# Side jobs of a feed-forward block cut into small pieces, part of them moved to the second block

## The chip, the cores and the metric

The kernel runs on one core of a Trainium2 chip. The metric is the device time of one execution in microseconds (us), smaller is better; the median of 3 runs before the change is 2384.21 us (2381.77 to 2387.19).

The engines of the core are called as in the profile: PE (TensorE, matrix products; PEld is its loading of the stationary operand), DVE (VectorE), ACT (ScalarE), POOL (GpSimd), SP (SyncE, which here only issues DMAs). Each engine works through its own queue in order. Line numbers such as L526 are those of the kernel before.

## The reference

A trunk of four layers over one sequence of 512 positions and 1024 channels, all in float32. Each layer is `x = x + mixer(rmsnorm(x))` and then `x = x + ffn(rmsnorm(x))`, and a last rmsnorm follows:

- layer 0 and layer 3: an S5 mixer, a diagonal complex state space of 64 groups (16 channels, 64 states each), followed by gelu and a gated product with a 1024 x 2048 weight;
- layer 1: gated linear attention (4 heads, chunks of 64);
- layer 2: differential attention with partial rotary embedding, 8 pairs of heads;
- each ffn: `(silu(h @ Wg) * (h @ Wu)) @ Wd` with 2816 hidden channels.

```python
def swiglu_ffn(h, w_gate_up, w_down):
    g, u = jnp.split(h @ w_gate_up, 2, axis=-1)
    return (jax.nn.silu(g) * u) @ w_down
```

The S5 mixer needs, from its small parameters alone and not from the sequence, matrices that bring each group's input into the states and out again, and the cosines and sines of the states' phases. The attention needs tables from the positions alone: rotary cosines and sines, chunk numbers, and the factor lambda. Work of this kind can be done at any time before its layer.

## The kernel before

**Precision.** Large products are made from two parts of each operand, high and low: `high` (L345, on ACT) rounds a weight tile to its first part in a tile `whl`, `low` (L349, on DVE) subtracts to get the second. Three matmuls then give one product (`mm3`, L362, L363, L364: high by high, high by low, low by high). There are five `whl` tiles in rotation and three `wst` tiles into which SP loads raw weights.

**A feed-forward block** (`ffn`, one per layer) makes the gate and up products in 11 blocks of 256 hidden channels, each by seven half-size products (L526, results in a, c and d) and sums of weight quarters. Some of those sums are made by DMAs that accumulate (L562, POOL's queue): such an issue waits until the plain load below it has landed. The first two blocks follow an order written out by hand (the `plan`); from then on a scheduler orders the instructions of each engine. It simulates their times and, at each point, takes the instruction that was written earliest among those it believes ready; the engine then keeps that order whatever the real times are. Behind every 3 or 4 blocks comes a batch of down products: `gemm_b`, once for each half `d` of the output, with four accumulators `acc`; each step of two k loads and splits a weight tile and makes eight `mm3` (two k, four row tiles t). At the last k `add_x` (L509, DVE) adds the accumulator to x and frees it. The first block makes its batches after 3, 3, 3 and 2 blocks, the others after 4, 4 and 3.

**The jobs.** `self.jobs` is a generator. The code calls `next` on it once for each k of a down product and once behind a block, and each call writes out the next piece of the jobs. In the first feed-forward block the jobs are `diff_tables` (the attention's tables) and then `s5_spilled`, which prepares the second S5 in eight steps of four channel blocks. One step: load the raw matrices (POOL's queue, L1018, L1021); transpose and combine them (PE `cps`, L1048; DVE L1008 to L1010); place them into blocks (ACT L1066, L1089, L1193; PE `xps`, L1134, and `rps`, L1101); send a small matrix through DRAM to reorder it (L1117 writes `rd`, eight DMAs of L1126 read it back); compute the phases (`s5_phases`: ACT L1155, L1162 to L1164 and DVE L1156 to L1160); and spill the results to DRAM by four DMAs on POOL's queue (L1221 in, L1222 cs, L1223 out, L1224 map). The buffers of a step exist once, so that a step's writes wait for the spills of the step before. These tiles lie in rooms that the block has finished with; the profile names them `halves` and `gain`, after the first tile there.

**The second S5** (`s5_second`) starts with memsets on POOL: two tiles `in`, two tiles `out` (`zero_off`, L1080 and L1081). It loads the first spilled tiles on SP. Meanwhile `Chunks.finish` makes the row factors: sums on DVE (L253, L254), a power on POOL (L256), a copy on DVE (L259), a transpose on PE (L261); only then can DVE scale (L1267) and PE go on (L1279).

Of the kernel before, what the change touches and what calls it, by code (L numbers as in the profile page):

```python
# [21 lines left out]
P = 128  # L22
# [203 lines left out]
class Chunks:  # L226
# [21 lines left out]
    def finish(self):  # L248
# [7 lines left out]
        nc.gpsimd.tensor_tensor(r[:], ms[:], tr.mhalf[:, :NT], op=ALU.pow)  # L256
# [12 lines left out]
class Trunk:  # L269
    def __init__(self, ctx, tc, ins, out):  # L270
# [22 lines left out]
        self.jobs = iter(())  # L293
        self.pend = []
# [48 lines left out]
    def high(self, w, a, n):  # L343
        hl = self.wp.tile([P, 2, a, n], F32R, tag="whl", name="whl", bufs=5)
        self.nc.scalar.copy(hl[:, 0], w[:])  # L345
        return hl

    def low(self, hl, w):
        self.nc.vector.tensor_tensor(hl[:, 1], w[:], hl[:, 0].bitcast(F32), op=ALU.subtract)  # L349
# [10 lines left out]
    def mm3(self, out, lh, ll, rh, rl, first, last):  # L360
# [3 lines left out]
        mm(out, ll, rh, start=False, stop=last)  # L364

    def gemm_b(self, stat, w, nk, c0, evac, k0=0, tail=0, between=(), ahead=None):
# [5 lines left out]
        done = 0  # L372
# [158 lines left out]
    def seven_block(self, fp, slots, left, wgu, b, turn, na):  # L531
# [118 lines left out]
        def four_out():  # L650
# [4 lines left out]
            for th, k in enumerate(("r1", "r5")):  # L655
# [6 lines left out]
                for j in range(2) if turn else (slice(None),):  # L662
                    nc.scalar.copy(dst[:, 0, j], src[:, j])
                    v.tensor_tensor(dst[:, 1, j], src[:, j], dst[:, 0, j].bitcast(F32), op=ALU.subtract)  # L664
# [7 lines left out]
    def ffn(self, l, left, after=None, turn=False, aside=None):  # L672

        i = self.i
# [3 lines left out]
        with self.tc.tile_pool(name=f"ffn{l}", bufs=1, reuse_waits="tile") as fp:  # L678
# [64 lines left out]
            else:  # L743

                self.jobs = iter(())
                slots[:] = [F[0], F[1], slots[0], F[2], left.g[:].rearrange("p (k n) -> p k n", n=256), F[3]] + slots[1:]
            b0 = 0
            for nb in (4, 4, 3) if na == 4 else (3, 3, 3, 2):
                acts = []
                for n in range(b0, b0 + nb):  # L750
# [13 lines left out]
                    if n > 2:  # L764
                        next(self.jobs, None)
# [3 lines left out]
                for d in range(2):  # L769
                    tail = 4 if d == 1 and b0 + nb == 11 else 0  # L770
                    self.gemm_b(stat, wd, 2 * nb, d * 512, self.add_x(d, nxt, r), k0=2 * b0, tail=tail)
# [374 lines left out]
    def s5_phases(self, pool, tag, L, kk, cs):  # L1146
# [7 lines left out]
        for b in range(4):  # L1154
            nc.scalar.activation(g2[:, b], self.mrow[:], AF.Identity, scale=col("f", b), bias=self.magic[:])  # L1155
        v.tensor_scalar_add(g2, g2, -MAGIC)  # L1156
        for b in range(4):
            v.scalar_tensor_tensor(g1[:, b], self.mrow[:], col("fhi", b), g2[:, b], op0=ALU.mult, op1=ALU.subtract)
            v.scalar_tensor_tensor(g1[:, b], self.mrow[:], col("flo", b), g1[:, b], op0=ALU.mult, op1=ALU.add)
        v.tensor_scalar(g1, g1, -0.5, 0.5, op0=ALU.max, op1=ALU.min)  # L1160
        ca = g1.rearrange("p b m -> p (b m)")
# [12 lines left out]
    def s5_spilled(self, pool, L):  # L1174
# [4 lines left out]
        cs = pool.tile([P, 2, 512], F32, name="cssp")  # L1179
# [5 lines left out]
        self.spill = []  # L1185
        self.dq = nc.gpsimd
        raw = self.s5_loads(pool, L, 0, 4)
        yield
# [6 lines left out]
        for kk in range(8):  # L1195
            bb, craw = raw
            ps = self.s5_qt(craw)
            X, one, two = self.s5_x(nc.vector, pool, L, 4 * kk, 4, bb)
            one()
            two()  # L1200
            yield
            Q, base, one, two = self.s5_q(nc.vector, pool, L, 4 * kk, 4)
            base(ps)
            one()
            two()
            self.s5_b_pads(bp, X, True)
# [3 lines left out]
            rv = self.s5_rows(4, bp, Q)  # L1210
# [4 lines left out]
            self.s5_map(L, 4 * kk, 4, rv, rs, mp, True)  # L1215
            x1 = self.s5_xt(X, 1, 0)
            yield
            diag(inm[:, 1], x1)
            d = [self.dp.tile([P, n], F32, name=f"{w}{kk}") for w, n in (("in", 512), ("cs", 1024), ("out", 512), ("map", 256))]
            flat = lambda y: y.rearrange("p a b c -> p (a b c)")  # L1220
            nc.gpsimd.dma_start(d[0][:], flat(inm))  # L1221
            nc.gpsimd.dma_start(d[1][:], cs.rearrange("p a b -> p (a b)"))  # L1222
            nc.gpsimd.dma_start(d[2][:].rearrange("p (z b n) -> p z b n", z=2, b=4), Q[:, :, :, 1:5].rearrange("p z b j h -> p z b (j h)"))  # L1223
            nc.gpsimd.dma_start(d[3][:], mp.rearrange("p b n -> p (b n)"))  # L1224
# [920 lines left out]
```

## Time and profile before

| | |
|---|---|
| median of 3 runs | 2384.21 us (2381.77 to 2387.19) |
| the profiled execution's own time | 2373.16 us |
| its span, first to last instruction | 2371.5 us |
| mean granted clock of PE | 0.981 |
| busy in the span | PE 94%, DVE 67%, ACT 47%, POOL 14% |

The profile shows one execution. A row of a group of instructions gives the line, the engine, the operation, the tiles written `<-` read, shapes and count, then the busy time in us and the mean of one in ns, then the idle time of the engine just before them and what ended it. A row of waits gives who waited for whom: us in total, times, longest. A row of the timeline gives start, duration, engine, line, operation, tiles, count, and in brackets the idle time before it with what ended it. PE's rows overlap, since matmuls are pipelined. The granted clock is the share of its full clock that PE was given.

### The profile page before, as it was taken

Reading aid. Unit: us, or ns where it says so; the run is one execution under the profiler, and the core shown is the slowest. Engines: PE = TensorE matmul, PEld = TensorE weight load, DVE = VectorE, ACT = ScalarE, POOL = GpSimd, SP = SyncE. Lnnn points to the kernel's source line nnn. Section 1 sums busy time; section 2 is a strip of 40 time slices with the busy share of each in tenths; the row PEclk is TensorE's granted clock in tenths of the full one; section 3 lists DMA queues with packets and bytes.
Section 4 is the critical chain, followed back from the end, with each engine's and each line's share of the span. In section 5 each row is a group of like instructions: output and inputs, shape, how many; then the busy total and the mean of one; then the engine's idle time right before and its main releaser. Section 6 shows DMA issues by size and latency. Waiting matters only on the chain. (4 is left out here: it accounts for less than half of the span.)

```text
span 2371.5 us, 37198 instructions
## 1 busy us (share of the span) xinstructions
PE 2238.7 (94%) x14847; PEld 1979.6 (83%) x14847; DVE 1582.2 (67%) x2416; ACT 1119.5 (47%) x1790; POOL 333.7 (14%) x417
## 2 busy tenths in 40 slices
PE   4799989999999999999999998999999799999997
PEld 3578978898977789898987787989989698999996
DVE  7764678886743559585753566885857774967674
ACT  3463545564553346253544576653534233634442
POOL 3330104334000011000001221110000100101000
PEclk9799999999999999999999999999999899999999
DMA  4124656676233257575345564895732446666621
GB/s 110 36 51 146 168 147 173 187 190 163 84 99 90 80 142 196 144 176 133 105 142 114 117 134 111 207 247 125 191 98 81 111 138 151 169 180 153 166 76 68
DMA packets 291719, 320.17 MB, mean 135 GB/s; under 512 B 68005, under 2 KB 231097, under 8 KB 291290
## 3 DMA queue, kind: packets, MB, share of 16 engines
q1 hardware_dynamic: 229434, 236.57, 32.6%
q0 software_dynamic: 62112, 81.22, 18.4%
q8 instruction: 117, 1.92, 0.3%
q14 instruction: 56, 0.46, 0.1%
HBM read 285.88 MB, written 16.65 MB: 128 GB/s over the span
## 5 line engine op out<-in xcount | busy, mean ns | idle before, releaser
L349 DVE TENSOR_TENSOR whl<-wst,whl 128x1024 fp32r<-128x1024 f32 x272 | 332.2, 1223 | 324.6 <-ACT whl L345 324.1
L345 ACT CAST whl<-wst 128x1024 fp32r<-128x1024 f32 x272 | 285.6, 1052 | 389.0 <-PE acc L364 291.7
L526 PE MATMUL a<-side,whl 128*128 128x256 f32 x3168 | 387.4, 279 | 12.1 <-ACT whl L345 7.5
L526 PEld LDWEIGHTS a<-side,whl 128*128 128x128 f32 x3168 | 374.4, 190 | 14.4 <-ACT whl L345 8.3
L362 PE MATMUL acc<-whl,act 128*128 128x512 f32 x704 | 279.5, 397 | 7.8 <-DVE g L571 3.2
L363 PE MATMUL acc<-whl,act 128*128 128x512 f32 x704 | 276.1, 392 | 0.0
L364 PE MATMUL acc<-whl,act 128*128 128x512 f32 x704 | 276.0, 392 | 0.0
L526 PE MATMUL c<-side,whl 128*128 128x256 f32 x2112 | 256.3, 278 | 5.1 <-DVE whl L349 5.1
L526 PEld LDWEIGHTS c<-side,whl 128*128 128x128 f32 x2112 | 248.9, 189 | 5.8 <-DVE whl L349 5.8
L349 DVE TENSOR_TENSOR whl<-slot,whl 128x1024 fp32r<-128x1024 f32 x105 | 127.9, 1222 | 64.8 <-ACT whl L345 64.6
L362 PEld LDWEIGHTS acc<-whl,act 128*128 128x128 f32 x704 | 133.0, 189 | 38.9 <-DVE g L571 4.1
L364 PEld LDWEIGHTS acc<-whl,act 128*128 128x128 f32 x704 | 133.0, 189 | 28.7 <-DVE act L664 0.5
L363 PEld LDWEIGHTS acc<-whl,act 128*128 128x128 f32 x704 | 133.2, 189 | 26.2
L345 ACT CAST whl<-slot 128x1024 fp32r<-128x1024 f32 x105 | 109.8, 1053 | 81.5 <-PE acc L364 45.8
L362 PE MATMUL acc<-whl,hT 128*128 128x512 f32 x352 | 142.3, 404 | 3.2 <-DVE ro L1870 1.5
L363 PE MATMUL acc<-whl,hT 128*128 128x512 f32 x352 | 137.4, 390 | 0.9 <-DVE whl L349 0.9
L364 PE MATMUL acc<-whl,hT 128*128 128x512 f32 x352 | 137.6, 391 | 0.0
L526 PE MATMUL d<-sides,whl 128*128 128x256 f32 x1056 | 133.6, 283 | 1.3 <-ACT whl L345 1.3
L526 PE MATMUL a<-sides,whl 128*128 128x256 f32 x1056 | 134.0, 283 | 0.0
L526 PEld LDWEIGHTS d<-sides,whl 128*128 128x128 f32 x1056 | 128.9, 191 | 2.1 <-ACT whl L345 1.9
L526 PEld LDWEIGHTS a<-sides,whl 128*128 128x128 f32 x1056 | 129.6, 191 | 1.0 <-ACT whl L345 0.2
L562 POOL DMA_DIRECT2D wst<-in_ffn_w_gate_up_dram x44 | 57.0, 1296 | 490.8 <-DMA wst<-in_ffn_w_gate_up_dram 292.2
(442 smaller groups left out, 3980.9 us busy)
## 6 DMA issues: line engine op xcount, KB each, us to landing
wst<-in_ffn_w_gate_up_dram SPq DMA_DIRECT2D x88, 512.0 KB, 3.9
wst<-in_ffn_w_down_dram SPq DMA_DIRECT2D x88, 512.0 KB, 4.5
slot<-in_ffn_w_gate_up_dram SPq DMA_DIRECT2D x69, 512.0 KB, 5.4
wst<-in_ffn_w_gate_up_dram POOLq DMA_DIRECT2D x44, 512.0 KB, 6.0
halves<-in_ffn_w_gate_up_dram SPq DMA_DIRECT2D x42, 512.0 KB, 5.9
wst<-in_s_w_glu_dram SPq DMA_DIRECT2D x32, 512.0 KB, 4.0
wst<-in_gla_w_in_dram SPq DMA_DIRECT2D x24, 512.0 KB, 3.6
wst<-in_diff_w_qkv_dram SPq DMA_DIRECT2D x24, 512.0 KB, 3.8
```

The lines of the kernel that those rows point to most:

```text
L345: self.nc.scalar.copy(hl[:, 0], w[:])
L349: self.nc.vector.tensor_tensor(hl[:, 1], w[:], hl[:, 0].bitcast(F32), op=ALU.subtract)
L362: mm(out, lh, rh, start=first, stop=False)
L363: mm(out, lh, rl, start=False, stop=False)
L364: mm(out, ll, rh, start=False, stop=last)
L526: mm(o, hl[:, x, k, c], side[:, y, k], start=first and not (j or k or n), stop=k == 3 and n == 2, skip_group_check=True,)
L562: nc.gpsimd.dma_start(w[:], left.quarter(*plus, b), accum_op=ALU.add)
```

## The change

- `gemm_b` takes `jobs=True` in the feed-forward blocks that have jobs. It then splits the weights of the next two k before the matmuls of the present two, and calls the jobs once behind every `mm3` (24 or 32 times in a down product) instead of once for each k. The call behind each block goes.
- `job()` writes out a piece with its instructions tied: on PE behind the last `mm3`, on ACT behind the last `high` or the last split of an activation, on DVE behind the last `low` or the like. The scheduler can't take them earlier than these. POOL and SP have no tie.
- The pieces are smaller: 17 for each of the eight steps of `s5_spilled`, and more `yield`s in the tables and the phases.
- The phases leave `s5_spilled`. A new generator `s5_phases_spilled` computes and spills them, each group in a `whl` tile of its own. It and `diff_tables` become the jobs of the second feed-forward block (`small`).
- In the second S5 the memsets of `out` come in the first step of the pipeline, tied behind the power.

The diff, cut to its core:

```diff
-        nc.gpsimd.tensor_tensor(r[:], ms[:], tr.mhalf[:, :NT], op=ALU.pow)
+        self.pow = nc.gpsimd.tensor_tensor(r[:], ms[:], tr.mhalf[:, :NT], op=ALU.pow)
...
+        self.last = {}
...
-        self.nc.scalar.copy(hl[:, 0], w[:])
+        self.last["high"] = self.nc.scalar.copy(hl[:, 0], w[:])
...
+    def job(self):
+
+        with ExitStack() as c:
+            for y in self.last.values():
+                c.enter_context(self.tc.issue_after(y.ins))
+            return next(self.jobs, None)
...
-        mm(out, ll, rh, start=False, stop=last)
+        self.last["mm"] = mm(out, ll, rh, start=False, stop=last)
...
         for kb in range(0, nk - tail, 2):
-            hl = self.wb(w, k0 + kb, c0)
+            hl = nxt or self.wb(w, k0 + kb, c0)
+            nxt = self.wb(w, k0 + kb + 2, c0) if jobs and kb + 2 < nk - tail else None
...
                 k = kb + a
-                if k:
-                    next(self.jobs, None)
...
                     if k == nk - 1:
                         evac(t, accs[t])
+                    if jobs:
+                        self.job()
...
                     acts.append(b["four_out"]())
-                    if n > 2:
-                        next(self.jobs, None)
...
         for kk in range(8):
             bb, craw = raw
+            yield
             ps = self.s5_qt(craw)
             X, one, two = self.s5_x(nc.vector, pool, L, 4 * kk, 4, bb)
             one()
+            yield
+            yield
             two()
-            yield
...
-            self.s5_phases(pool, "gsp", L, kk, cs)
...
-            nc.gpsimd.dma_start(d[1][:], cs.rearrange("p a b -> p (a b)"))
...
+    def s5_phases_spilled(self, L):
+
+        for kk in range(8):
+            p = Slices(self.wp.tile([P, 2048], F32, tag="whl", name="phases", bufs=5))
+            cs = p.tile([P, 2, 512], F32, name="cssp")
+            yield from self.s5_phases(p, "gsp", L, kk, cs)
+            d = self.spill[kk]["cs"] = self.dp.tile([P, 1024], F32, name=f"cs{kk}")
+            self.nc.gpsimd.dma_start(d[:], cs.rearrange("p a b -> p (a b)"))
+            for _ in range(4):
+                yield
...
-            for y in (*ins, *outs):
+            for y in ins:
                 self.zero_off(y, 64, nc.gpsimd)
...
             def steps(kk):
+                if kk == 0:
+                    with self.tc.issue_after(left.pow.ins):
+                        for y in outs:
+                            self.zero_off(y, 64, nc.gpsimd)
...
-        def aside(fp):
+        def small():
             yield from self.diff_tables()
-            yield from self.s5_spilled(fp, 1)
-
-        left = self.ffn(0, left, i["norm_mix"][1], aside=aside)
+            yield from self.s5_phases_spilled(1)
+
+        left = self.ffn(0, left, i["norm_mix"][1], aside=lambda fp: self.s5_spilled(fp, 1))
         left = self.gla(1, left, i["norm_ffn"][1])
-        left = self.ffn(1, left, i["norm_mix"][2])
+        left = self.ffn(1, left, i["norm_mix"][2], small=small)
```

More of the change, by code (lines that the diff above doesn't have):

```diff
@@ L363, in mm3, with gemm_b @@
         mm(out, lh, rl, start=False, stop=False)
-        mm(out, ll, rh, start=False, stop=last)
-    def gemm_b(self, stat, w, nk, c0, evac, k0=0, tail=0, between=(), ahead=None):
+        self.last["mm"] = mm(out, ll, rh, start=False, stop=last)
+    def gemm_b(self, stat, w, nk, c0, evac, k0=0, tail=0, between=(), ahead=None, jobs=False):
         between = iter(between)
         accs = [self.acc() for _ in range(NT)]
-        done = 0
+        hl = nxt = None
         for kb in range(0, nk - tail, 2):
-            hl = self.wb(w, k0 + kb, c0)
+            hl = nxt or self.wb(w, k0 + kb, c0)
+            nxt = self.wb(w, k0 + kb + 2, c0) if jobs and kb + 2 < nk - tail else None
             if kb == 2:
@@ L662, in four_out @@
                 for j in range(2) if turn else (slice(None),):
-                    nc.scalar.copy(dst[:, 0, j], src[:, j])
-                    v.tensor_tensor(dst[:, 1, j], src[:, j], dst[:, 0, j].bitcast(F32), op=ALU.subtract)
+                    self.last["act high"] = nc.scalar.copy(dst[:, 0, j], src[:, j])
+                    self.last["act low"] = v.tensor_tensor(dst[:, 1, j], src[:, j], dst[:, 0, j].bitcast(F32), op=ALU.subtract)
             return act
@@ L670, in seven_block, with ffn @@
         )}
-    def ffn(self, l, left, after=None, turn=False, aside=None):
+    def ffn(self, l, left, after=None, turn=False, aside=None, small=None):
+        jobs = bool(aside or small)
         i = self.i
@@ L743, in ffn @@
             else:
-                self.jobs = iter(())
+                self.jobs = small() if small else iter(())
                 slots[:] = [F[0], F[1], slots[0], F[2], left.g[:].rearrange("p (k n) -> p k n", n=256), F[3]] + slots[1:]
@@ L1184, in s5_spilled @@
         nc.gpsimd.memset(rs[:, :, :48], 0.0)
-        self.spill = []
+        self.spill = [{} for _ in range(8)]
         self.dq = nc.gpsimd
         raw = self.s5_loads(pool, L, 0, 4)
-        yield
         def diag(dst, ps):
@@ L1486, in loads @@
                 if "out" in names:
-                    blocks(outs[kk % 2][:, :2], d[2], 2)
-                    blocks(outs[kk % 2][:, 2:], d[3], 1)
+                    blocks(outs[kk % 2][:, :2], d["out"], 2)
+                    blocks(outs[kk % 2][:, 2:], d["map"], 1)
             def steps(kk):
+                if kk == 0:
+                    with self.tc.issue_after(left.pow.ins):
+                        for y in outs:
+                            self.zero_off(y, 64, nc.gpsimd)
                 if kk + 1 < 8:
@@ L1762, in diff_tables @@
             v.tensor_copy(pf[:, 1], ci[:])
+            yield
+            yield
+            yield
             ps = self.tp("pps")
```

51 lines of the change are left out of this document (36 added, 15 removed).

## The prediction

> **What bounds the kernel now.** I read the page first, then each of the four feed-forward blocks as one stretch, then the waits of TensorE, then the rows around each wait. The page:
>
> ```profile
> span 2371.5 us, 37198 instructions
> PE 2238.7 (94%) x14847; PEld 1979.6 (83%) x14847; DVE 1582.2 (67%) x2416; ACT 1119.5 (47%) x1790; POOL 333.7 (14%) x417
> ```
>
> TensorE (PE) is busy for 94% of the span, so only its idle pieces (132.8 us in all) and what they cause can be won. The four feed-forward blocks, from the first product L526 to the last L364 of each (start:end length, then busy time of PE, PEld, DVE, ACT, POOL, the granted PE clock, DMA share and rate):
>
> ```profile
> 265.10:657.50 392.40, 372.37 (x2867) 336.10 (x2866) 314.88 (x559) 217.20 (x372) 103.70 (x156) 0.97 0.58 155
> 875.60:1218.70 343.10, 339.94 (x2417) 318.06 (x2416) 243.61 (x276) 162.84 (x209) 24.26 (x19) 1.00 0.55 143
> 1503.00:1847.00 344.00, 338.14 (x2391) 316.06 (x2390) 248.36 (x291) 165.64 (x223) 28.38 (x26) 0.99 0.58 152
> 2018.20:2358.20 340.00, 335.98 (x2391) 313.92 (x2389) 232.08 (x260) 152.22 (x186) 24.10 (x19) 1.00 0.51 135
> ```
>
> The same products take 392.4 us in the first block and 342.4 us (mean of the other three) elsewhere. The first is the one with the jobs beside it, and it pays 50.0 us for them. What the jobs themselves occupy on PE there, from the groups by line (busy us, mean ns, idle before):
>
> ```profile
> L1134 PE MATMUL xps<-ident,halves 64*64 64x64 f32 x256 | 11.8, 236 | 1.0 <-ACT halves L1193 1.0
> L1048 PE MATMUL cps<-ident,halves 128*64 128x128 f32 x64 | 5.3, 285 | 0.0
> L1101 PE MATMUL rps<-halves 128*32 128x64 f32 x128 | 4.2, 236 | 5.7 <-DVE neglam L1793 4.7 <-DVE halves L1010 1.0
> L1765 PE MATMUL pps<-ident,dtab 4*128 4x4 f32 x2 | 0.3, 209 | 0.0
> ```
>
> That is 11.8 + 5.3 + 4.2 + 0.3 = 21.6 us. The other 50.0 - 21.6 = **28.4 us** are waiting and its after-effects, and they are what this change can reach. PE's waits in the first block, and in the second for comparison:
>
> ```profile
> PE rps L1101 <- DVE neglam L1793: 4.7, 1, 4.7
> PE a L526 <- ACT whl L345: 3.6, 1, 3.6
> PE acc L362 <- DVE x L509: 2.6, 1, 2.6
> PE acc L362 <- DVE g L571: 2.4, 1, 2.4
> PE acc L362 <- ACT act L663: 2.0, 1, 2.0
> PE a L526 <- DVE whl L349: 1.0, 1, 1.0
> ...
> PE a L526 <- ACT whl L345: 2.0, 1, 2.0
> PE a L526 <- DVE whl L349: 0.8, 1, 0.8
> ```
>
> (The last two are the second block's; two more of 1.0 us each stand in the rows of L1134 and L1101 above.) A wait also costs clock. Stretches behind three of these waits, one behind the 2.6 us wait (575.30), and the one in the second block (915.00): length, PE busy, granted clock.
>
> ```profile
> 304.00:310.80 6.80, 5.84 (x28) 0.50 0.83 198
> 355.20:362.00 6.80, 5.20 (x40) 0.50 0.54 92
> 450.80:457.60 6.80, 6.12 (x28) 0.50 0.43 131
> 575.30:582.10 6.80, 6.80 (x57) 1.00 0.63 134
> 915.00:918.40 3.40, 3.40 (x19) 0.50 1.13 321
> ```
>
> Half clock for 6.8 us loses 3.4 us, for 3.4 us it loses 1.7 us.
>
> **The change part by part.**
>
> *1. The hold at 349 to 357 us.* Its origin, on ACT and DVE:
>
> ```profile
> 344.41 1.27 ACT L1155 ACTIVATE halves<-mrow,magic,s5f 128x128 f32<-128x128 f32 x3 [11.35 <-DMA cs<-halves]
> 346.66 1.22 DVE L349 TENSOR_TENSOR whl<-wst,whl 128x1024 fp32r<-128x1024 f32 x1 [9.33 <-ACT whl L345]
> ```
>
> A piece of the phases (L1155) stood at the head of ACT's queue for 11.35 us, until the table of the group before had left its single buffer, and a weight split (L345) stood behind it; DVE sat 9.33 us for that split and then met a pile of jobs. PE lost 2.0 + 4.7 + 1.0 = 7.7 us, and 3.4 us of clock: 11.1 us. The phases leave this block, and with them the single buffer; the attention tables (L1793 is their last step) leave as well. I take all 11.1 us as gone.
>
> *2. The wait at 449.5 us* has the same origin: L571 was late behind phases on DVE, with an L1155 again waiting for the same buffer. 2.4 + 1.0 + 3.4 = 6.8 us, gone.
>
> *3. The start, 303 us.* Jobs were drawn ahead into the order written out by hand: from 296.9 to 300.0 DVE ran pieces of them, the last one this.
>
> ```profile
> 299.50 0.62 DVE L1159 SCALAR_TENSOR_TENSOR gain<-mrow,s5flo,gain 128x128 f32<-128x128 f32 x2
> ```
>
> Tied behind the last split they can't be there. PE waits 3.6 + 1.0 here, 2.0 + 0.8 in the second block, which has no jobs: 1.8 us, and 3.4 - 1.7 = 1.7 us of clock: 3.5 us. The rest of this wait is the plan's own and stays.
>
> The 2.6 us wait for L509 stays in my sum: there DVE held S5 work behind a landing, and that S5 work stays in this block. So 21.4 of the 28.4 us go.
>
> *4. What stays in the first block* is 21.3 us of PE work in 32 groups (four per step of four blocks, eight steps), now one piece behind each third matmul of the down products: 17 pieces by 8 steps is 136, and there are 48 places in each of the first three batches, 144, so nothing is left for the end. At some 0.68 us for three matmuls a step takes 17 x 0.68 + 2.7 us = 14.3 us. Per step POOL must issue (groups by line, first block; the last row is the issue of rd alone, L1117, within the second batch's down products):
>
> ```profile
> L1126 POOL DMA_DIRECT2D halves<-rd x64 | 32.7, 519 | 27.0 <-DMA rd<-halves 26.3 <-DMA halves<-rd 0.4 <-issue 0.3
> L1223 POOL DMA_DIRECT2D out<-halves x8 | 8.4, 1048 | 4.8 <-DVE halves L1010 2.7 <-DVE gain L1158 2.0
> 445.00:492.00 47.00, 1.65 (x3) 0.93 0.60 158
> ```
>
> 8 x 0.52 + 1.05 + 1.65 / 3 is 5.8 us; six smaller issues, at rd's 0.55 to out's 1.05 each, are 3.3 to 6.3, and I take the lower part, 4; 26.3 / 8 = 3.3 us is the landing of rd. Together about 13 us of 14.3. POOL is the tightest of the queues; behind a late rd wait the next step's buffers, and behind those ACT and DVE pieces with weight splits after them. What softens it: the splits of the next two k now stand ahead of the jobs, about 5.4 us (8 x 0.68) of lead, and three steps already fit into one batch's 47 us (the x3 of the last row), with the phases beside them. Bounds for new waits here: nothing, and 16 us (half a microsecond on each of the 32 groups). I take 3.0 us, about one more wait like L509's, since three of 32 groups waited before.
>
> *5. The second block* receives the phases. Per group of four, by these rows of the first block:
>
> ```profile
> L1155 ACT ACTIVATE halves<-mrow,magic,s5f 128x128 f32<-128x128 f32 x32 | 14.0, 488 | 20.1 <-DMA cs<-halves 20.0
> L1164 ACT ACTIVATE halves<-gain,halfpi 128x512 f32<-128x512 f32 x8 | 5.8, 724 | 0.2
> L1159 DVE SCALAR_TENSOR_TENSOR gain<-mrow,s5flo,gain 128x128 f32<-128x128 f32 x32 | 10.6, 349 | 0.1
> 960.00:1005.00 45.00, 45.00 (x206) 37.50 (x206) 20.76 (x23) 10.42 (x11) 2.76 (x3) 1.00 0.47 125
> ```
>
> ACT 4 x 0.49 + 0.72 and two like it of 0.63 is 3.9 us, DVE 8 x 0.35 and two of 0.45 is 3.7 us, and one spill on POOL. The last row is the first batch of down products there: DVE busy 20.8 of 45.0 us, ACT 10.4. Some 4.5 groups fall into it, so DVE goes to 37 and ACT to 28 us of 45: covered by PE, with little room on DVE. Bounds: nothing, and one hold like part 1's, 11.1 us. I take 1.0 us, plus 0.3 us for the tables' two transposes on PE. If the cover failed altogether, DVE's 8 x 3.7 = 30 us would show.
>
> *6. The second S5.* Rows of POOL, DVE, PE and SP:
>
> ```profile
> 1848.26 0.62 SPq L1481 DMA_DIRECT2D cs<-cs  x1
> 1848.99 0.28 DVE L254 TENSOR_SCALAR ms<-ms 128x4 f32<-128x4 f32 x1
> 1849.30 0.73 POOL L1080 MEMSET out<- 64x768 f32 x1
> ...
> 1852.48 1.04 POOL L256 TENSOR_TENSOR rcol<-ms,mhalf 128x4 f32<-128x4 f32 x1
> ...
> 1853.84 0.47 PE L261 MATMUL rt<-ident,Rt 128*128 128x128 f32 x1 [5.13 <-DVE Rt L259]
> ...
> 1861.12 1.19 SPq L1473 DMA_DIRECT2D out<-out  x2
> ...
> cs<-cs SPq DMA_DIRECT2D x5, 512.0 KB, 4.3
> ```
>
> Its input was ready at 1849.27, but the power (L256) stood behind four memsets of out and began at 1852.48. Behind the memsets of in alone it begins at about 1849.35: **3.1 us**. The out memsets (four of 0.73) then end near 1853.4, and their tiles are loaded at 1861.12, so they stay hidden. What is late next is the first table cs, issued at 1848.26; these transfers take 4.3 us (last row, the median of five), so it lands near 1852.6; PE's new start is 1850.7, and the transpose, its copy, a scaling and the first product lie between that and the multiplication with cs, so I let the landing cost nothing. Bounds: nothing, and 6.5 us (with the clock piece behind it). I take 3.1.
>
> *Sum:* -11.1 - 6.8 - 3.5 + 3.0 + 1.3 - 3.1 = **-20.2 us**. The profiled execution took 2373.16 us for its span of 2371.5; that makes 2353.0 us. The median of the runs shown, 2384.2 us, lies 11.0 us above the profiled one; the same terms from there give **2364.0 us**, which is my forecast.
>
> [...]
>
> **The rivals.** *All of the jobs' cost beyond PE work goes* (28.4 us) and the second S5 gains 6.5: 2384.2 - 34.9 = 2349 us. For it: the other blocks run so. Against it: L509's wait has its cause still in place.
>
> *Waits move into the job groups.* A piece on DVE now stands behind the split of the next weights, and that split behind a weight's landing; PE takes its job group in order, so a late weight stops PE at a job. With 16 us for 3.0 in part 4: 2384.2 - 20.2 + 13.0 = 2377 us. For it: POOL's 13 of 14.3 us. Against: only three of 32 groups waited, with more work beside them.
>
> *The ties don't do what they are for.* They keep a job from running early; they don't take a stuck job off the head of a queue. If ACT's and DVE's S5 pieces wait for landings as L1155 did, holds 1 and 2 come back and only parts 3 and 6 count: -3.5 - 3.1 + 1.3 = -5.3, 2379 us.
>
> *Slower: the weight slots in the second block.* Each group of phases borrows one of the five weight slots until its spill has landed, and that spill stands on POOL behind accumulating loads that wait for landings. The 64 places of the first batch end inside the fifth group, which keeps its slot through four blocks of products. Where a split must wait for such a slot, the price is a hold like part 1's, 11.1 us. Without part 5's 1.0 us the sum is -21.2: two holds give 2385 us, three give 2396; from the second on nothing is left of the gain. For it: L1155 waited 20.0 us in total for spills. Against: four slots remain, for products of 2.7 us each against a split of 1.05 + 1.22 us.
>
> **How the numbers follow.** Forecast 0.48 (own range 2355 to 2373), everything goes 0.12, waits in job groups 0.16, ties without effect 0.10, slots 0.14. Less than 0.2% (4.8 us) can't be told from no change: 2379.4 to 2389.0. Faster: 0.48 + 0.12, with 0.7 of 0.16 and half of 0.10: 0.76. Slower: 0.09, the three-hold part of the slots. Same: 0.15. The range 2350 to 2386 leaves out about half of the best case and most of the slots' worst.
>
> **What would show it.** Right: the first block's stretch falls from 392.4 to about 374 us, no L1155 and no L1793 in it, no half-clock stretch behind the first down products, the second block stays within 2 us of 343, and L256 starts under 0.3 us after L254 ends. Wrong: PE waits on xps, rps or cps for DVE or ACT add up to more than 8 us (waits moved); ACT's L345 in the second block waits on a landing of the phases' spill (slots); L509 waits in each batch (POOL's queue sets the pace).

## The result, and the profile after

The changed kernel takes 2362.83 us (median of 4 runs, 2357.91 to 2366.1), the kernel before 2383.25 us (4 runs beside it): ratio 0.991, 95% interval 0.9886 to 0.9934, that is 16 to 27 us less. A second set (6 runs against 12) gave 2360.93 against 2376.27 us, ratio 0.9933, 0.9912 to 0.9955. The forecast was 2364.0 us.

The page of the changed kernel; it answers to the page's lines shown of before:

```profile
span 2364.4 us, 37216 instructions
...
PE 2245.8 (95%) x14847; PEld 1985.6 (84%) x14847; DVE 1586.0 (67%) x2416; ACT 1119.2 (47%) x1790; POOL 332.3 (14%) x417
```

The profiled execution took 2366.1 us. Its span is only 7.1 us under that of before, far less than the medians differ, so the stages are compared one by one. The first two feed-forward blocks of the changed kernel (start:end length, busy time of PE, PEld, DVE, ACT, POOL, granted clock, DMA share and rate), then its first stage, up to the first block, and its second S5:

```profile
272.20:645.60 373.40, 365.98 (x2865) 330.01 (x2863) 290.56 (x438) 191.47 (x314) 98.83 (x148) 1.00 0.60 152
866.90:1213.90 347.00, 342.15 (x2419) 319.46 (x2418) 270.02 (x397) 189.45 (x267) 28.76 (x27) 0.99 0.58 154
...
0.00:272.20 272.20, 217.11 (x1425) 173.83 (x1425) 165.57 (x310) 117.65 (x199) 70.93 (x71) 0.91 0.38 95
1839.40:2009.80 170.40, 156.13 (x924) 137.39 (x923) 114.81 (x157) 53.70 (x84) 11.91 (x21) 0.95 0.54 139
```

The first stage and the second S5 of the kernel before:

```profile
0.00:265.10 265.10, 209.55 (x1425) 166.90 (x1425) 165.05 (x310) 117.97 (x199) 72.04 (x71) 0.94 0.38 98
1847.00:2018.20 171.20, 156.41 (x924) 137.59 (x923) 114.01 (x157) 53.94 (x84) 11.90 (x21) 0.95 0.52 139
```

The reader is to see three things. The first block went from 392.4 to 373.4 us (-19.0), the second from 343.1 to 347.0 (+3.9), the second S5 from 171.2 to 170.4 (-0.8): -15.9 us in the stages that the change touches. In the profiled execution of the second set they are 372.9, 345.5 and 170.4, -17.9 us. And the first stage, which has the same instructions in the same order on every engine in both kernels, took 7.1 us longer at a granted clock of 0.91 instead of 0.94: that hid a good part of the gain in this one execution.

The first block falls into two parts with different troubles. Its start, in the order written out by hand, is taken here up to a `d` product that waits some 0.44 us for a split; it is the same product in all kernels (at 319.51 before, at 323.94 in the changed one). The start went from 54.4 to 51.7 us. The rest, before and changed:

```profile
319.50:657.50 338.00, 322.92 (x2466) 287.25 (x2467) 264.13 (x483) 181.79 (x321) 94.39 (x145) 0.98 0.59 159
323.90:645.60 321.70, 317.43 (x2464) 282.26 (x2465) 244.13 (x383) 158.53 (x271) 91.16 (x139) 1.00 0.60 152
```

So 2.7 of the 19.0 us were won at the start and 16.3 behind it.

PE's waits in the first block and then in the second, changed kernel (us in total, times, longest; a last one of 0.4 us, alike in both, is left out):

```profile
PE a L535 <- ACT whl L346: 2.0, 1, 2.0
PE acc L370 <- DVE g L580: 1.9, 1, 1.9
PE xps L1143 <- DVE halves L1019: 1.3, 1, 1.3
PE xps L1143 <- ACT halves L1204: 0.9, 1, 0.9
PE a L535 <- DVE whl L350: 0.8, 1, 0.8
...
PE a L535 <- ACT whl L346: 2.0, 1, 2.0
PE a L535 <- DVE x L518: 1.6, 1, 1.6
PE a L535 <- DVE whl L350: 0.8, 1, 0.8
...
```

(L535 is the product called L526 before, L370 the first of `mm3`, L346 and L350 the splits, L580 the gain's line L571, L518 the addition L509, L1143 the `xps` transposes.) The waits of 4.7 us of `rps`, 2.6 for x and 2.0 for act are gone, and that for the first weight split is 2.0 instead of 3.6 us; the start of the first block waits exactly as that of the second does. The 1.6 us for x in the second block are new.

### The profile page after: what moved, and what is told of

The parts are those of the page before. It is cut to its first block, busy times and chain, and to the rows that moved or that the text cites. A ratio compares the mean times of both kernels' runs of the same rounds, so it can differ in the third digit from the quotient of the medians.

```text
span 2364.4 us, 37216 instructions
## 1 busy us (share of the span) xinstructions
PE 2245.8 (95%) x14847; PEld 1985.6 (84%) x14847; DVE 1586.0 (67%) x2416; ACT 1119.2 (47%) x1790; POOL 332.3 (14%) x417
## 5 line engine op out<-in xcount | busy, mean ns | idle before, releaser
L350 DVE TENSOR_TENSOR whl<-wst,whl 128x1024 fp32r<-128x1024 f32 x272 | 332.1, 1223 | 310.2 <-ACT whl L346 309.6
L346 ACT CAST whl<-wst 128x1024 fp32r<-128x1024 f32 x272 | 285.2, 1050 | 383.2 <-PE acc L372 265.5
L535 PE MATMUL a<-side,whl 128*128 128x256 f32 x3168 | 388.7, 280 | 9.0 <-ACT whl L346 5.9
L535 PEld LDWEIGHTS a<-side,whl 128*128 128x128 f32 x3168 | 375.9, 191 | 11.0 <-ACT whl L346 7.1
L370 PE MATMUL acc<-whl,act 128*128 128x512 f32 x704 | 278.2, 395 | 3.0 <-DVE g L580 3.0
L535 PE MATMUL c<-side,whl 128*128 128x256 f32 x2112 | 255.8, 278 | 4.3 <-DVE whl L350 4.3
L535 PEld LDWEIGHTS c<-side,whl 128*128 128x128 f32 x2112 | 248.6, 189 | 4.7 <-DVE whl L350 4.7
L350 DVE TENSOR_TENSOR whl<-slot,whl 128x1024 fp32r<-128x1024 f32 x105 | 127.9, 1223 | 66.4 <-ACT whl L346 65.9
L370 PEld LDWEIGHTS acc<-whl,act 128*128 128x128 f32 x704 | 132.1, 188 | 33.2 <-DVE g L580 4.2
L370 PE MATMUL acc<-whl,hT 128*128 128x512 f32 x352 | 143.4, 407 | 2.1 <-DVE ro L1918 1.5
L346 ACT CAST whl<-slot 128x1024 fp32r<-128x1024 f32 x105 | 110.0, 1052 | 73.9 <-PE acc L372 28.2
L535 PE MATMUL a<-sides,whl 128*128 128x256 f32 x1056 | 134.0, 283 | 1.6 <-DVE x L518 1.6
L535 PE MATMUL d<-sides,whl 128*128 128x256 f32 x1056 | 133.5, 283 | 1.3 <-ACT whl L346 1.3
L535 PEld LDWEIGHTS a<-sides,whl 128*128 128x128 f32 x1056 | 129.4, 191 | 2.7 <-issue 2.0
L535 PEld LDWEIGHTS d<-sides,whl 128*128 128x128 f32 x1056 | 128.9, 191 | 2.0 <-ACT whl L346 1.9
L571 POOL DMA_DIRECT2D wst<-in_ffn_w_gate_up_dram x44 | 56.8, 1290 | 445.7 <-DMA wst<-in_ffn_w_gate_up_dram 257.1
```

The source lines that it names most:

```text
L346: self.last["high"] = self.nc.scalar.copy(hl[:, 0], w[:])
L350: self.last["low"] = self.nc.vector.tensor_tensor(hl[:, 1], w[:], hl[:, 0].bitcast(F32), op=ALU.subtract)
L370: mm(out, lh, rh, start=first, stop=False)
L535: mm(o, hl[:, x, k, c], side[:, y, k], start=first and not (j or k or n), stop=k == 3 and n == 2, skip_group_check=True,)
L571: nc.gpsimd.dma_start(w[:], left.quarter(*plus, b), accum_op=ALU.add)
```

## The experiments

Each kernel's time stands beside runs of the kernel before on the same chip: 2380.16 us (23 runs) for 1, 2, 3 and 9; 2379.54 us (17) for 4, 6, 7 and 8; 2376.27 us (12) for 5, 10, 11 and 12, which is the changed kernel again. Block times are from one profiled execution of each kernel. "Theory H" is the prediction's own reason, that the phases and the tables leave the first block; theory T holds the ties and small pieces for the cause. Line numbers differ by a few from kernel to kernel.

**1. The changed kernel without ties.**

```diff
 def job(self):
-    with ExitStack() as c:
-        for y in self.last.values():
-            c.enter_context(self.tc.issue_after(y.ins))
-        return next(self.jobs, None)
+    return next(self.jobs, None)
```

> The changed kernel without the ties: the pieces are as small and the splits as far ahead, but the scheduler may take a piece as early as it believes it ready. Theory H (the gain is that the phases with their single buffer and the tables left the first block; the ties only keep the start clean): the wait at the start of the first block comes back, 3.5 us, the first block's stretch goes from 373.4 to about 377 us, the time from 2362.8 to about 2366. Rival T (the ties and the small pieces make the gain): the stretch goes back by 15 us or more, to about 390, the time to about 2378.

Measured: 2370.98 us, ratio 0.9961 (0.9944 to 0.9978): by the medians 9.2 us of the 15 to 20. Its first block, and PE's longest waits there:

```profile
270.60:650.20 379.60, 367.44 (x2865) 331.58 (x2864) 291.06 (x439) 191.76 (x314) 98.81 (x148) 0.98 0.56 149
```

```profile
PE acc L368 <- DVE g L578: 4.0, 1, 4.0
PE a L533 <- ACT whl L346: 3.3, 1, 3.3
PE cps L1055 <- DMA halves<-in_s_c_re_dram: 2.5, 1, 2.5
```

Without ties a transposition of the jobs (`cps`) stands in PE's queue before its raw matrix has landed, and the first wait, 3.3 us, is nearly the old one of 3.6. What follows: with the phases gone from the block, 6.2 us of its 19.0 still hang on the ties, and all of them at the start. It takes 58.8 us instead of 51.7, with 24 of the jobs' instructions on PE drawn into it; the rest is no longer than in the changed kernel:

```profile
329.40:650.20 320.80, 316.80 (x2440) 282.31 (x2441) 240.53 (x365) 156.24 (x261) 88.58 (x135) 0.99 0.57 152
```

**2. The phases back in the first block**, all else as changed (ties, small pieces, splits ahead); the old single buffer for cs is back too.

```diff
+        cs = pool.tile([P, 2, 512], F32, name="cssp")
...
             rv = self.s5_rows(4, bp, Q)
+            for _ in self.s5_phases(pool, "gsp", L, kk, cs):
+                pass
             yield
...
+            nc.gpsimd.dma_start(d["cs"][:], cs.rearrange("p a b -> p (a b)"))
...
-            yield from self.s5_phases_spilled(1)
```

> The changed kernel with the phases back in the first block, in the steps, with one buffer for all of them as before; ties, small pieces, splits ahead, moved tables and moved memsets stay. Theory H: L1155's wait for the spill of the step before stands at the head of ACT's queue again, one or two holds of 7 to 11 us come back, the first block's stretch goes to 383 to 392 us, the second block's falls from 347.0 to about 344, the time to 2370 to 2380. Rival T: the ties keep the splits ahead of such a piece, the stretch grows by 4 us at most, to 377, and the time by 1 us.

Measured: 2362.35 us, ratio 0.9922 (0.9895 to 0.9949), as the changed kernel. Blocks, and what the first activation of the phases (called L1155 before) waited for in the first block:

```profile
271.80:645.70 373.90, 366.85 (x2865) 330.56 (x2863) 311.28 (x519) 218.40 (x370) 104.03 (x156) 1.00 0.60 163
867.00:1211.60 344.60, 341.58 (x2418) 319.15 (x2417) 248.02 (x316) 163.27 (x211) 24.26 (x19) 0.99 0.54 143
```

```profile
L1164 ACT ACTIVATE halves<-mrow,magic,s5f x32: 477/481/497, 345.1 to 578.7; 128x128 f32<-128x128 f32 x32
...
  DMA cs<-halves: 2.7, 2
```

DVE and ACT again do the phases in this block (311.28 and 218.40 us busy, as before), and the block keeps its 373.9 us. The single buffer, which held ACT for 20.0 us before, holds it for 2.7. So phases and buffer need not leave the block, as theory H had it. (The tables stay moved here.)

**3. The move alone:** the kernel before with only the phases and the tables moved, each group in a `whl` tile; no ties, old pieces and calls.

```diff
-            self.s5_phases(pool, "gsp", L, kk, cs)
...
+        def small():
+            yield from self.diff_tables()
+            yield from self.s5_phases_spilled(1)
...
-        left = self.ffn(1, left, i["norm_mix"][2])
+        left = self.ffn(1, left, i["norm_mix"][2], small=small)
```

> The kernel before with one edit alone: phases (each group in a weight slot of its own) and tables become jobs of the second block; no ties, pieces as large as before, no splits ahead, memsets as before. Theory H: holds 1 and 2 (11.1 and 6.8 us) go, the first block's stretch falls from 392.4 to about 375 us, the second block's grows from 343.1 to 345 to 348, the time falls from 2383 to about 2368. Rival T: the first block keeps at least two thirds of its 28.4 us, 385 us or more, and the time stays above 2376.

Measured: 2381.84 us, ratio 1.0012 (0.9996 to 1.0029). The blocks, and a piece of DVE's queue in the second:

```profile
268.40:652.30 383.90, 368.91 (x2864) 334.58 (x2863) 290.21 (x438) 190.50 (x315) 98.99 (x148) 0.97 0.56 147
870.30:1229.30 359.00, 346.45 (x2419) 319.14 (x2418) 269.55 (x397) 189.10 (x267) 28.70 (x27) 0.99 0.55 149
```

```profile
956.17 0.29 DVE L1795 TENSOR_TENSOR dtab<-dtab 128x128 f32<-128x128 f32 x1 [3.68 <-DMA dtab<-in_diff_lam_k_dram]
956.38 0.68 DVE L643 TENSOR_TENSOR r<-c,r 128x512 f32<-128x512 f32 x1
```

The first block wins 8.5 us, the second loses 15.9. There a step of the tables (L1795) stood at the head of DVE's queue for 3.68 us, for a vector that had not landed, and the block's own L643 stood behind it. The cost went along with the work.

The first block, though, shows more than its sum. Its start is 5.5 us longer (59.9 for 54.4: a `cps` of the jobs waits 2.8 us there, the first product after it 5.2). Its rest is 14.0 us shorter than before:

```profile
328.30:652.30 324.00, 318.23 (x2456) 284.96 (x2457) 239.71 (x365) 155.66 (x264) 88.74 (x135) 0.99 0.57 151
```

So behind the start the move alone does what theory H says. What H left out is the start and the second block.

**4. The ties alone:** the kernel before with `job()` and `self.last` at the old calls, with the old coarse pieces; nothing moved.

```diff
-                    next(self.jobs, None)
+                    self.job()
```

(at both calls, with `job()` itself and the lines that set `self.last`.)

> The kernel before with the ties alone: every piece of a job is tied behind the last split, act and product built so far, at the old call places and with the old coarse pieces; nothing is moved, no split is ahead, the memsets stay first. Theory T (the ties make the gain): the waits at craw, at the spill of cs and at the start of the first stage's end go, the first block's stretch falls from 392.4 to 375 to 380 us, the time to 2365 to 2371. Rival P (ties on coarse pieces only put a long piece in one lump behind the last product, where the next split waits behind it): the hold at the single buffer of cs, 11.35 us, stays to within 3 us, the stretch is 387 to 395 us, the time 2376 to 2386.

Measured: 2374.80 us, ratio 0.9985 (0.9972 to 0.9999): by the medians 4.7 us of the 15 to 20. The first block, then rows of ACT, DVE and PE in it:

```profile
274.50:665.50 391.00, 373.61 (x2867) 336.77 (x2865) 313.85 (x559) 218.23 (x372) 103.22 (x156) 0.97 0.59 156
```

```profile
375.05 1.65 ACT L1163 ACTIVATE halves<-mrow,magic,s5f 128x128 f32<-128x128 f32 x4 [7.23 <-DMA cs<-halves]
376.60 1.03 ACT L346 CAST whl<-slot 128x1024 fp32r<-128x1024 f32 x1
376.73 0.43 DVE L1164 TENSOR_SCALAR halves<-halves 128x512 f32<-128x512 f32 x1 [5.16 <-ACT halves L1163]
...
379.27 0.42 DVE L1018 TENSOR_TENSOR halves<-halves 128x256 f32<-128x256 f32 x1
379.83 0.39 PE L1109 MATMUL rps<-halves 128*32 128x64 f32 x2 [4.59 <-DVE halves L1018]
```

This is the old hold over again, now tied in place: the phases (L1163, L1155 before) wait on ACT for the single buffer (7.23 us), a weight split stands behind them, DVE sits and then has a whole coarse piece to do, and PE stands at `rps` (L1109), whose source is the end of that piece (4.59 us, and 4.2 us in another place). A tie fixes the earliest place of an instruction and does nothing for one that arrives there before its source. The start of the block takes 51.8 us, as with all kernels that have ties; the rest gains nothing:

```profile
326.30:665.50 339.20, 324.98 (x2466) 288.94 (x2467) 267.35 (x504) 185.22 (x329) 95.41 (x147) 0.97 0.59 159
```

**5. Ties and small pieces, no split ahead, phases in the first block.**

```diff
-            nxt = self.wb(w, k0 + kb + 2, c0) if jobs and kb + 2 < nk - tail else None
+            nxt = self.wb(w, k0 + kb + 2, c0) if False else None
```

(and the edit of experiment 2.)

> The changed kernel with the phases back in the first block's steps and no split ahead: what is left of the change is the ties, the small pieces, the later memsets and the tables in the second block. Theory B (ties and small pieces work only together: a tie alone puts a transposition right behind a product while its source on DVE is still to come, a small piece alone is drawn ahead): nearly the whole gain, the first block's stretch 373 to 377 us, the second 343 to 346, the time 2358 to 2366. Rival A (the parts add up: small pieces without ties won about 9 us, ties without small pieces about 5, splits ahead about 6): without the splits ahead about 14 us are left, the first block's stretch 377 to 381, the time 2365 to 2370.

Measured: 2358.50 us, ratio 0.9936 (0.9913 to 0.9958), against 0.9933 of the changed kernel beside it. The second block takes 344.6 us by the same view; the first:

```profile
267.20:641.90 374.70, 366.84 (x2865) 330.65 (x2864) 311.13 (x519) 218.47 (x371) 103.52 (x156) 1.00 0.61 162
```

The start takes 51.6 us, and the rest:

```profile
318.80:641.90 323.10, 318.38 (x2464) 282.79 (x2465) 264.59 (x463) 185.47 (x328) 95.67 (x147) 1.00 0.61 166
```

Ties and small pieces together make nearly the whole gain in this block, with about the same DVE work in it as before (311 us for 315), as theory B expects.

But the two parts of the block answer to different things. The ties win the start: 51.6 to 51.8 us in every kernel that has them, 54.4, 58.8 and 59.9 without (before, experiments 1 and 3). Behind the start, small tied pieces win 14.9 us with the phases in place (323.1), the move alone 14.0 (324.0), ties on coarse pieces nothing (339.2).

Small pieces without ties and with the phases in place were not run. Nor was the effect of the tables by themselves: they stay in the first block in experiment 4 and leave it in 2 and 5. In 4 they cost PE one wait of 2.8 us, against 8.8 us of waits at `rps`.

**6. No split ahead, phases in the second block** (the one-line edit of 5 alone).

> The changed kernel, but a weight tile of the down product is split when its own products come, as before, and not one tile ahead; ties, small pieces and moves stay. Theory T (what cost time was pieces of jobs that the scheduler drew in front of the blocks' own instructions; the ties alone end that): the split is then late only by what stands before it, waits of the up products on a weight tile's split (a from whl) stay near the 3.2 us of the changed kernel's first block, its stretch is 373 to 376 us, the time within 3 us of the changed kernel (2360 to 2366). Rival S (the splits ahead carry the gain: a tie to the latest split means nothing if the split itself is late): waits of products on split tiles are 6 to 10 us in the first block, its stretch 379 to 384 us, the time 2368 to 2376.

Measured: 2366.04 us, ratio 0.9946 (0.9931 to 0.9961); the two kernels of the same batch that keep the splits ahead (7 and 8) took 2360.26 and 2359.75. The first block takes 373.0 us by the same view; the second, and the longest of PE's waits in it that the changed kernel doesn't have:

```profile
864.40:1214.90 350.50, 342.11 (x2419) 317.55 (x2418) 269.50 (x397) 189.86 (x267) 28.70 (x27) 1.00 0.57 153
```

```profile
PE acc L370 <- ACT whl L346: 1.6, 1, 1.6
```

Neither theory as written: the first block doesn't need the splits ahead (373.0 us), the second seems to when the phases are in it (350.5 us in this one profile, against 347.0 and 345.5 in two with them).

**7. Four pieces in a lump once for each k**, instead of one behind each `mm3`.

```diff
-                    if jobs:
-                        self.job()
+                    if jobs and t == NT - 1:
+                        for _ in range(NT):
+                            self.job()
```

> The changed kernel with its pieces drawn four in a lump behind the last product of each k, where it draws one behind each group of three products; ties, splits ahead and moves stay. Theory T (order of the jobs against the blocks' own work is all that counts, the ties give it in either case): the same within 3 us, the first block's stretch 373 to 377 us, 2360 to 2366. Rival P (small pieces are the cure: a lump of four holds ACT or DVE for 2 to 4 us when the next split or addition is due): waits of products on splits and gains 3 us or more longer in each of the first two blocks, the first block's stretch 378 to 384 us, 2368 to 2378.

Measured: 2360.26 us, ratio 0.9927 (0.991 to 0.9943); blocks 374.1 and 345.1 us, by the same view. Theory T holds: where within a k the pieces are called is of little matter, about 1 us in the first block. So "small" in experiment 5 means a step cut into 17 pieces and spread over a little more than four k, not their being behind each `mm3`. Nor are small phases meant: in experiments 2 and 5 all phases of a step are in one piece.

**8. The memsets of out before the power again.**

```diff
-            for y in ins:
+            for y in (*ins, *outs):
                 self.zero_off(y, 64, nc.gpsimd)
```

(and without the tied ones.)

> The changed kernel with the memsets of the out tiles in front of the pow of the second S5, as before the change. The prediction's part 6: the pow starts 3.1 us later again and the stage is 3.1 us longer, 173.5 us for 170.4, the time 3.1 us above the changed kernel (2366). Rival G (the gain at the pow is given back at the copies of r4 that stand ahead of the gelu on ACT): the pow starts 3 us later, the wait of zp for ACT is shorter by about as much, the stage is 170 to 171.5 us, the time within 1 us of the changed kernel.

Measured: 2359.75 us, ratio 0.9925 (0.991 to 0.994); the second S5 171.3 us instead of 170.4. PE's wait for the factors is back, 5.1 us for 2.6. The 7.1 us that PE waits in the changed kernel at `zp` (the transposes behind the gelu) are gone; PE idles 4.8 us ahead of a product V (L1311) instead, which the profile puts down to no other engine. Two rows of the second S5 of this kernel, then rows of the changed one:

```profile
1836.26 0.28 DVE L254 TENSOR_SCALAR ms<-ms 128x4 f32<-128x4 f32 x1
...
1839.74 1.05 POOL L256 TENSOR_TENSOR rcol<-ms,mhalf 128x4 f32<-128x4 f32 x1
```

```profile
1841.39 0.28 DVE L254 TENSOR_SCALAR ms<-ms 128x4 f32<-128x4 f32 x1
...
1841.80 1.05 POOL L256 TENSOR_TENSOR rcol<-ms,mhalf 128x4 f32<-128x4 f32 x1
...
1862.31 1.06 PE L1342 MATMUL y<-out,prods 128*128 128x128 f32 x8
...
1864.57 0.62 ACT L1516 COPY cs<-s5r 128x512 f32<-128x512 f32 x1 [11.20 <-DVE mods L1330]
...
1869.20 0.62 ACT L1516 COPY cs<-s5r 128x512 f32<-128x512 f32 x1 [4.01 <-DVE mods L1330]
...
1871.13 0.60 ACT L1344 ACTIVATE room<-y 128x512 f32<-128x512 f32 x1
...
1871.78 1.12 PE L1353 MATMUL zp<-ident,room 128*128 128x128 f32 x4 [6.63 <-ACT room L1344]
```

The power starts 3.2 us after L254 here and 0.13 us after it in the changed kernel, so the edit does what it says. But in the changed kernel two copies of r4 (L1516) stand ahead of the gelu (L1344) on ACT, waiting 11.20 and 4.01 us for scans on DVE; the last products before the gelu are done near 1863.4, and PE waits 6.63 us for it. In the kernel of this experiment the later of the two stands behind the gelu, so it is the scheduler's new order that gives the gain back. Rival G holds: of 3.1 us, 0.9 is kept.

**9. The copies of r4 on POOL**, all else as changed.

```diff
-                    nc.scalar.copy(r4, self.k5["r4"][:, c : c + 4].unsqueeze(2).broadcast_to([P, 4, P]))
+                    nc.gpsimd.tensor_copy(r4, self.k5["r4"][:, c : c + 4].unsqueeze(2).broadcast_to([P, 4, P]))
```

> The changed kernel with the copies of r4 in the second S5 made by POOL instead of ACT. In the changed kernel such a copy, which waits for DVE's scans, stands on ACT ahead of the first gelu, and PE waits 6.6 us for that gelu. Theory G (this order gives the 3.1 us of the moved memsets away): the wait of 6.6 us falls to 2 us or less, the stretch between the third and the fourth feed-forward block goes from 170.4 to about 167 us, the time from 2362.8 to about 2360. Rival D (DVE is the limit of that stage, and PE waits there in any case): the wait moves to another place, the stretch stays at 170 to 171 us, the time within 1 us.

Measured: 2357.09 us, ratio 0.9905 (0.988 to 0.993). The second S5 took 168.9 us, 1.5 less. The wait of 6.6 us is gone, and this one is new:

```profile
PE acc L371 <- DVE whl L350: 4.7, 1, 4.7
```

So both theories in part: the copies held the gelu, and with them gone a weight split, late on DVE, takes most of it.

**10. Phases back in the first block and r4 on POOL** (the edits of 2 and 9).

> The changed kernel with the phases back in the first block's steps and the copies of r4 of the second S5 on POOL instead of ACT. If the two edits add up: the second block's stretch 344 to 346 us instead of 347, the second S5 168 to 170 instead of 170.4, together 3 to 5 us under the changed kernel, 2355 to 2359. If POOL, which takes the copies beside the memsets and the gather of the tables, holds the spilled loads back: the second S5 170 to 173 us and no gain, 2360 to 2364.

Measured: 2356.55 us, ratio 0.991 (0.9885 to 0.9935), the lowest median of its batch, 4.4 us under the changed kernel there. The blocks and the second S5 take 374.4, 344.7 and 169.0 us by the same view: +1.5, -0.8 and -1.4 against the changed kernel beside it. So its stages account for less than 1 us; the rest of the difference of the medians is not shown to be the edits'. Their runs overlap (2350.45 to 2361.4 and 2356.45 to 2366.89).

**11. As 10, with sums on POOL** for the first four k of the second S5.

```diff
-            e = v if L else nc.gpsimd
+            e = v if L and kk > 3 else nc.gpsimd
```

> As the kernel with phases back and r4 on POOL, and for the first four k of the second S5 the sum and the difference of the products of V and cs are on POOL instead of DVE. If DVE, busy without a hole from the end of the up products' scaling to the first split of a weight tile, bounds the start of that stage: eight instructions of 0.68 us leave it and the stage falls by 2 to 5 us, to 164 to 167 us, the time by as much. If POOL's own instruction (its time for this shape is in no row of this stage) and the two hand-overs are longer than what DVE saves, the scans start later: the stage 169 to 173 us, the time the same to 4 us longer than that kernel's.

Measured: 2360.51 us, ratio 0.9929 (0.9909 to 0.995); the second S5 171.3 us, 2.3 longer than in 10. The two sums on POOL, and PE's longest wait in that stage:

```profile
L1324 POOL TENSOR_TENSOR mods<-mods 128x512 f32<-128x512 f32 x4 | 6.4, 1601 | 0.0
L1323 POOL TENSOR_TENSOR mods<-mods 128x512 f32<-128x512 f32 x4 | 5.1, 1268 | 9.0 <-DVE mods L1320 9.0
```

```profile
PE V L1316 <- DVE mods L1319: 5.8, 1, 5.8
```

On average 1.27 and 1.6 us for a sum that takes 0.68 on DVE, and the scans behind it start later: eight instructions fewer on DVE shorten the wait for the split from 4.7 to 4.0 us, and the wait for `mods` grows from 3.1 to 5.8.

**12. The changed kernel again.**

> The changed kernel as it is, on the same chip and beside the same runs of the kernel before as the other kernels of this batch. Any theory: 2359 to 2365 us, first block's stretch 373 to 375 us. What differs from its first profile in stages with the same order of instructions is the clock: if it is, the first stage lies anywhere from 265 to 272 us.

Measured: 2360.93 us, as told above; the first stage took 272.0 us.

## Why the prediction was right, and where it was not

The time was right, to 1.2 us; that it is so near is luck, since the two sets of runs themselves differ by 5 us in the gain. The sum, -20.2 us, lies inside the first interval (-27 to -16) and near the edge of the second (-21 to -11); the stages of the two profiles give -15.9 and -17.9. So it is a few us too large: parts 5 and 6 were too hopeful, and the first block a little better than forecast (-19.0 for -18.4).

*Parts 1 and 2, the two holds: the size right, the reason enough but not needed.* "The phases leave this block, and with them the single buffer; the attention tables leave as well" was the reason given for 17.9 us. Experiment 3 makes only the move, and behind the start the block wins 14.0 of the 16.3 us of the changed kernel. Experiments 2 and 5 put phases and buffer back and win 15.8 and 14.9 us there (322.2 and 323.1 us for 338.0): cut small and tied, the same work in the same place doesn't hold the block either. The changed kernel has both cures, so its own result can't tell them apart. What the two remove is the same: an instruction that comes in one lump with its own source, or whose source is late, stands at the head of ACT's, DVE's or PE's queue while the block's work stands behind it (11.35 us on ACT before, 3.68 on DVE in experiment 3, 4.59 on PE in experiment 4). The wait at 449.5 us was misread in one point: DVE had no phases ahead of L571 there; it sat 2.35 us for ACT's L663, which stood behind an L1155 that waited 2.58 us. One term was also too generous: in the first batch of down products a wait of 1.9 us stays, now for g (L580), where the 2.0 us for act of part 1 stood; by the same view it is 2.7 and 3.7 us in experiments 5 and 7.

*Part 3, the start: right.* It waits 2.0 and 0.8 us as in the second block; without ties the 3.3 us are back. The start is 2.7 us shorter, for 3.5 forecast, and it is the only part of the block for which the ties are shown to be needed.

*The wait of 2.6 us for x, left in the sum: wrong,* it went too. *Part 4, the first block's remainder: right by its sum.* 3.0 us were allowed for new waits; waits at `xps` are 1.3 + 0.9 = 2.2 us, and the block's excess over other blocks and its job work on PE (11.2 + 5.3 + 3.9 = 20.4 us by the view by lines) is 373.4 - 342.4 - 20.4 = 10.6 us against the forecast 28.4 - 21.4 + 3.0 = 10.0. POOL did not set the pace: PE has no wait for x (L518) in this block.

*Part 5, the second block: too small.* +1.3 forecast, +3.9 and +2.4 measured in two profiles. The sign "stays within 2 us of 343" was missed. Its own start, up to the same product as above, is 1.1 us longer in the first of these profiles, before any job, where the half clock lasts 6.8 instead of 3.4 us (0.50 over 904.30 to 911.13). Behind it the block takes 291.5 us before, 292.1 and 292.0 with the tables alone (experiments 2 and 5), and 294.2 in both profiles of the changed kernel. So the tables cost about half a microsecond and the phases about 2, of which PE's new wait for x (1.6 us) is the most: the addition stands on DVE behind phases and splits. The first block gains about 1 us by the phases' absence (373.4, 373.0, 372.9 and 374.1 against 373.9, 374.7 and 374.4). Beside ties and small pieces the move of the phases is worth nothing, then, and without the splits ahead the one profile shows some 4 us more lost.

A row of ACT's waits in the second block of the changed kernel is that of the slot rival:

```profile
ACT whl L346 <- DMA cs<-phases: 6.6, 2, 4.8
```

Its mechanism is there, but PE's waits for splits in this block are the same 2.0, 0.8 and 0.4 us as before.

*Part 6, the second S5: the gain at the power right, the term wrong.* 3.1 us became 0.9, since what is late next was looked for in the landing of cs; it is the gelu behind ACT's copies of r4. Bounds of 0 to 6.5 had held it.

*The rivals.* "The ties don't do what they are for" names what experiment 4 shows behind the start: on coarse pieces "holds 1 and 2 come back". That this kernel's gain of 4.7 us is near the rival's 5.3 is chance, since those count parts 5 and 6, which it doesn't have. What the rival missed is that cutting the step, or moving the phases, cures that. "All goes" needed the second S5's 6.5 us; "waits in job groups" is refuted by the 2.2 us.

*The base.* Taking the sum from the median and not from the profiled execution was right only because the profile of before was a quick one: 2373.16 us, where runs of it beside the experiments go from 2365.94 to 2387.65.

*The clock.* At the start of the first block of the changed kernel waits of 2.0 and 0.8 us, with matmuls between them, are still followed by half the clock (0.50 granted over 310.40 to 313.80; a row around that place):

```profile
307.00:320.60 13.60, 10.88 (x78) 10.63 (x78) 13.21 (x17) 7.42 (x10) 1.34 (x1) 0.87 0.73 175
```

A granted 0.87 over 13.60 us is about 3.5 us at half speed, as part 3 left it.

**What stays open.** Why, on coarse tied pieces, two steps of the S5 work come so close that the single buffer is still being spilled, was not isolated; nor was which of the cuts within a step matters, what small pieces do without ties when the phases stay, and what the tables' move is worth in the first block. The split of the block into start and rest comes from one execution of each kernel (two of the changed one). The medians of near kernels differ by 2 to 4 us, and none of the versions above is shown to beat the changed one beyond its interval.

## What to carry to other kernels

Before moving side work to another stage because a wait names it, try the same work in the same place, cut into smaller pieces and tied behind the main work: here that won as much of the block as the move did (14.9 and 14.0 us behind its start), and the move brought a cost of its own to the other block, 15.9 us in coarse untied pieces and some 2 us in small tied ones. Look at the parts of a stage one by one: ties won the start of the block, and cutting or moving the rest. Which cuts matter is not shown; the phases of a step were in one piece in experiments 2 and 5 without loss. When a stall at a stage's start is removed, follow each engine's queue to the next thing that the stage waits for, since an instruction in order behind another's wait can give the gain back (2.2 of 3.1 us in experiment 8). And compare stages, not spans, when single executions are set side by side.

## What had not been expected of the hardware

The first stage, with the same order of instructions, took 265.0 us in the quickest and 274.5 us in the longest of these profiles. The kernel with r4 on POOL and that with the ties alone (start:end length, busy times, granted clock):

```profile
0.00:265.00 265.00, 209.48 (x1423) 166.89 (x1424) 165.86 (x310) 117.85 (x199) 71.01 (x71) 0.94 0.39 98
```

```profile
0.00:274.50 274.50, 216.72 (x1425) 173.24 (x1425) 164.50 (x310) 117.70 (x199) 73.11 (x71) 0.89 0.37 95
```

DVE and ACT are busy for nearly the same time, PE 7.2 us longer at 0.89 instead of 0.94. These 9.5 us between two executions of the same instructions are as large as most of the effects studied here.

A copy of 128x512 and two sums of that shape cost POOL 1.09, 1.27 and 1.6 us on average in experiment 11, such a sum on DVE 0.68.
